# Compressed keys with the tokens held stationary, computed behind the first gates; their probabilities split in two ahead of the transposes

## The chip, the cores and the metric

The kernel runs on one core of one Trainium2 chip. The core has a tensor engine (PE in the profile, with its weight loads listed apart as PEld), VectorE (DVE), ScalarE (ACT), GpSimd (POOL), and SyncE (SP), whose queue issues all the DMAs of this kernel. Each engine works through its own queue in order and waits on semaphores of the others. The metric is the device time of one execution in microseconds (us).

## The reference

Two layers of a decoder trunk over 512 tokens of width 1024, in float32. In each layer one projection feeds four mixers; the outputs are gated, concatenated, projected and added to the residual. The change touches mixer B, which has three branches: attention over compressed blocks of keys, over selected blocks, and over a window. With 512 tokens, 16 selected blocks of 64 and a window of 512, the second and third branch see every earlier token. The compressed branch is this:

```python
cmp_idx = cmp_start[:, None] + jnp.arange(CMP_LEN)[None, :]      # 31 blocks of 32 tokens, 16 apart

def compress(tok, w):
    blocks = tok[:, cmp_idx] + pe_cmp
    return blocks.reshape(B, n_cmp, CMP_LEN * HEAD_DIM) @ w

k_cmp = rope(compress(kc_tok, w_cmp_k)[:, :, None], cmp_end, ROT_DIM)[:, :, 0]
v_cmp = compress(vc_tok, w_cmp_v)
...
s_c = jnp.einsum('bqhd,bnd->bhqn', qb, k_cmp) * scale
p_c = masked_softmax(s_c, valid_c)
o_c = jnp.einsum('bhqn,bnd->bqhd', p_c.astype(dtype), v_cmp)
...
return g[..., 0:1] * o_c + g[..., 1:2] * o_s + g[..., 2:3] * o_w
```

## The kernel before

Tokens are cut into four tiles of 128. Large products run in float32r; to keep float32 accuracy both operands are split into a high and a low part, and three of the four products are added (`lin_tok`, lines 137 to 139, with the tokens stationary; `lin_ch`, lines 147 to 149, with the weights stationary and all 512 tokens moving). Weights come in groups through four staging buffers `st`; ACT rounds them to the high part `wh` (line 122), POOL subtracts to get the low part `wl` (line 95).

A layer first runs the projections of queries, keys, values and of an indexer, as a software pipeline over tiles. Then come, in the order of the source: `compress`, the gates of mixer A (`gates("a", 0)`, `gates("a", 1)`), the gates of mixer B, attention of both mixers tile by tile with the top-k search `topk` (lines 341 and 342, long chains of MAX8 and MATCH_REPLACE8 on DVE) and the convolution and pooling mixers in between, and last the output projection.

The order within each engine's queue is not the order of the source. A list scheduler places the instructions by its own estimate of time, with the source's order as priority; so a change of one step can move rows far from it, and rows of later steps fill the gaps of earlier ones.

`compress` projects the tokens to compressed-branch keys and values (one `lin_ch`). It loads the position term `pe_cmp` by a DMA, transposes it on PE (line 443) and copies it to `pe` on DVE (line 445). ACT copies the projection into two buffers `u` (one for keys, one for values) in which each column holds a token and the token 16 further on; POOL adds `pe` to each (line 463). Then line 467 multiplies: for keys and for values 16 products each, with a 128x64 piece of the weight `st` stationary and 32 columns of `u` (every 16th) moving, into 64 rows of a bank `ms`. These are float32 products, and the profile lists each as two instructions. ACT copies the result to `kv`, PE transposes it back (line 473), and ACT and DVE make `zc` (keys, rotated in lines 262 to 265) and `vc` (values, high and low part, 32 rows). `zc` is transposed (line 480) into the first 32 columns of the window keys `kTB`.

In `att_b(i)` the 32 compressed probabilities of four heads end up in `e` (128 tokens x 4 x 32). Line 590 transposes each head's 32 columns; ACT rounds the 32x512 result to `ph` (line 593), DVE subtracts to get `pl`, and two products with 32 rows each (lines 595 and 596) add to the bank `pv` that already holds the other two branches. Scores of a head (lines 509 and 510) go into one of two banks `s`; DVE reads them (line 513), ACT takes the exponential (line 515). A gate's `lin_ch` goes into one of two banks `mm`, which DVE frees with line 493.

Of the kernel before, what the change touches and what calls it, by code (L numbers as in the profile page):

```python
# [28 lines left out]
BIG = 10  # places for tiles of [P, T]  # L29
WARM = 28  # products on nothing at the start  # L30
# [4 lines left out]
# first columns of the parts of w_in  # L35
A_Q, A_V, A_QI, A_KI, A_GATE, B_Q, B_KC, B_KS, B_GATE, C_B, C_GATE = 0, 320, 384, 640, 680, 936, 1192, 1320, 1588, 1844, 2612

# columns of the table of shape constants
# [27 lines left out]
def trunk(ctx: ExitStack, tc: tile.TileContext, x, norm_w, w_in, w_out, conv_w, pe_cmp, w_cmp_k, w_cmp_v,  # L66
# [26 lines left out]
    def lo(eng, dst, src, hi):  # L93
        """dst = src - hi, the part of src that its rounding to float32r left out."""
        eng.tensor_sub(dst, src, f(hi))  # L95

# [1 line left out]
    def load_w(src, segs, early=None, start=False):  # L98
        """segs: (first column, columns) runs of src that make up one group; by quarters of its rows.
        early: tag of a place that is still free for the loads; start: the first group of all"""  # L100
# [28 lines left out]
    def lin_tok(ps, act, i, w, c0, n, order=range(KC)):  # L129
        """ps[:, :n] = act (tokens of tile i) @ w[:, c0:c0+n]"""  # L130
# [10 lines left out]
    def lin_ch(act, w, c0):  # L141
        """(w[:, c0:c0+128])^T @ act^T : 128 channels by all tokens"""
# [31 lines left out]
    # the tensor engine's clock rises only after some microseconds of work: done on nothing while the loads run  # L174
# [13 lines left out]
    psh = const.tile([P, DEPTH, 2], F32, name="psh")  # L188
    x1d = dp.tile([T, DM], F32, name="x1d")

    def first_loads(h):
        """the other loads, between those of the first group of weights"""
# [25 lines left out]
    def mean_sq(xp, acc):  # L218
        """acc (EPS to begin with) and the part of the mean of squares that the columns xp make up"""
# [9 lines left out]
    def rms(xt, g, ms=None):  # L229
        """xt, g: by halves of the columns; ms: mean of xt's squares"""  # L230
# [21 lines left out]
    def rope(eng, z, n, half, tb, rows=P):  # L252
        """z: [rows, n, d], rotated in place; tb: [rows, 4*half] = cos, cos, -sin, sin"""
# [13 lines left out]
    def pipeline(tasks, depth=4):  # L267
        """Starts a task with each round, and takes each of those under way a step further."""
# [17 lines left out]
    def layer(l, hT, w_first, norm):  # L286
        """hT: the layer's normalized input, transposed, w_first: its first group of weights; norm, if any, writes
        the tiles of hT. Returns the like for the next layer."""
# [12 lines left out]
        def group_idx(i, w):  # L301
            """indexer queries of tile i, and the scores of its tokens against those before"""
# [8 lines left out]
            # rows of qiT[h % 4]: high, high, low part of the queries; of kiT: high, low, high part of the keys  # L311
# [37 lines left out]
        # keys of the selected and of the window branch; the compressed ones stand before the latter  # L349
# [4 lines left out]
        def stack_q(m, i, pq):  # L354
            """pq: two heads a transpose; even heads as (high, low), odd ones as (low, high) rows"""
# [61 lines left out]
        def group_bq(i, w):  # L417
            """queries of the second mixer, values of the first"""
# [16 lines left out]
        kcT = [kTB[s][:, 1, 0:32] for s in range(2)]  # L435
        vc = res.tile([32, P], F32R, name=nm("vc"), tag="vc")

        def compress(w):
# [6 lines left out]
            V.tensor_copy(pe, pt[:, 0:16])  # L445
            pc = bank("ms", 1)
            us = []
            wts = []
            for s, wsrc in enumerate((w_cmp_k, w_cmp_v)):
# [14 lines left out]
                us.append(u)  # L464
            for s in range(2):
                for t in range(16):
                    PE.matmul(pc[0:HD, s * 32 : (s + 1) * 32], wts[2 * s + t // 8][:, t % 8, :], us[s][:, t::16],  # L467
                              start=t == 0, stop=t == 15)
            kv = sm.tile([HD, 2, 32], F32, name=nm("kv"), tag="kv", bufs=1)
# [86 lines left out]
        def att_b(i):  # L556
# [32 lines left out]
            for h in range(NH):  # L589
                PE.transpose(pt[0:32, h * P : (h + 1) * P], e[:, h, :], ident)  # L590
# [200 lines left out]
```

## Time and profile before

| | |
|---|---|
| median of 3 runs | 576.3 us (573.21 to 577.37) |
| span of the profiled execution | 577.7 us; no time of it outside the span is listed |
| busy: PE, PEld, DVE, ACT, POOL | 542.4, 473.1, 448.9, 318.3, 296.0 us |
| DMA | 51.14 MB, mean 89 GB/s |
| HBM | 46.33 MB read, 4.19 MB written |

The profile is one execution; times in it are us from the start of the span unless marked ns. Busy time of PE is modelled and overlaps (matmuls are pipelined), so the distance between the starts of two matmuls is the better measure of what one costs. The chain of waits follows the work that ended last back from the end. A view of windows gives, for each stretch of time, how long each engine was busy and the clock that PE was granted, as a share of full speed.

### The profile page before, as it was taken

The page shows a single profiled execution, that of the slowest core. Times are in us where ns is not written, and L with a number is a line of the kernel's source. Part 1 is how long each engine was busy: PE and PEld are TensorE (multiplying, and loading weights), DVE is VectorE, ACT ScalarE, POOL GpSimd, SP SyncE. Part 2 cuts the span into 40 slices and gives each one's busy share as a digit, 9 for nine tenths or more (in the row PEclk, how much of TensorE's full clock was granted, in tenths as well). Part 3 has the DMA queues.
Part 4 walks back from the last instruction along what each step waited for, and adds up shares of the span by engine and source line. Part 5 has one row for each costly group of instructions (what it writes and reads, how often), then busy time and mean ns, then how long its engine had stood idle before and what let it go on. Part 6 is the DMA issues. An engine that isn't in the chain of part 4 may idle for free.

```text
span 577.7 us, 9703 instructions
## 1 busy us (share of the span) xinstructions
PE 542.4 (94%) x3088; PEld 473.1 (82%) x3088; DVE 448.9 (78%) x1154; ACT 318.3 (55%) x787; POOL 296.0 (51%) x394
## 2 busy tenths in 40 slices
PE   5989799798999999999999989989999999999995
PEld 4989697676878877699999978768788887869895
DVE  4867899799999977762275769987999997897523
ACT  3457855253547566663455595536454756565433
POOL 4755641364546194643675455326554639273342
PEclk9899999799999999999999999987999999999999
DMA  8632311283222020526531512116513212123303
GB/s 260 192 94 54 74 34 23 56 209 83 54 56 65 28 79 13 147 91 198 147 117 48 141 35 64 37 37 178 134 30 81 64 48 58 52 88 114 111 1 145
DMA packets 70370, 51.14 MB, mean 89 GB/s; under 512 B 19248, under 2 KB 64432, under 8 KB 70320
## 3 DMA queue, kind: packets, MB, share of 16 engines
q1 hardware_dynamic: 70320, 50.54, 31.8%
q8 instruction: 24, 0.39, 0.3%
q14 instruction: 26, 0.21, 0.1%
HBM read 46.33 MB, written 4.19 MB: 87 GB/s over the span
## 4 chain that ended last, share of the span: by engine, by line
PE 67%; DVE 22%; ACT 4%; POOL 2%; issue 2%; DMA 2%; SPq 1%; POOLq 0%; ACTq 0%; DVEq 0%
PE mm L139 9%; PE mm L137 9%; PE mm L138 8%; PE mm L147 7%; PE mm L148 7%; PE mm L149 7%; PE tr L529 4%; DVE acc L342 4%; DVE acc L331 4%; DVE m L341 3%; PE ms L467 2%; PE s L509 2%; PE s L510 2%; PE pv L535 2%; PE pv L534 2%
## 5 line engine op out<-in xcount | busy, mean ns | idle before, releaser
L95 POOL TENSOR_TENSOR wl<-st,wh 128x768 fp32r<-128x768 f32 (+4 forms) x94 | 159.2, 1713 | 63.2 <-ACT wh L122 51.2
L147 PE MATMUL mm<-hT,wh 128*128 128x512 f32 x272 | 110.1, 405 | 3.8 <-DVE sg L493 3.0
L149 PE MATMUL mm<-hT,wl 128*128 128x512 f32 x272 | 108.2, 399 | 0.0
L148 PE MATMUL mm<-hT,wh 128*128 128x512 f32 x272 | 108.1, 399 | 0.0
L522 POOL TENSOR_SCALAR pb<-pb,rs 128x512 f32<-128x512 f32 (+3 forms) x96 | 53.7, 577 | 98.8 <-DVE rs L519 39.0
L515 ACT ACTIVATE pb<-pb,mn 128x512 f32<-128x512 f32 (+3 forms) x96 | 53.7, 559 | 72.1 <-DVE mn L513 71.6
L122 ACT ACTIVATE wh<-st 128x768 fp32r<-128x768 f32 (+4 forms) x92 | 70.7, 775 | 25.4 <-DMA st<-in_w_in_dram 9.2
L137 PE MATMUL mm<-wh,hT 128*128 128x360 f32 (+3 forms) x240 | 74.8, 313 | 8.1 <-ACT hT L248 4.3
L139 PE MATMUL mm<-wh,hT 128*128 128x360 f32 (+3 forms) x240 | 74.7, 312 | 0.9 <-DVE hT L95 0.9
L138 PE MATMUL mm<-wl,hT 128*128 128x360 f32 (+3 forms) x240 | 74.1, 310 | 0.0
L147 PEld LDWEIGHTS mm<-hT,wh 128*128 128x128 f32 x272 | 51.8, 191 | 14.2 <-DVE sg L493 3.5
L137 PE MATMUL mm<-wh,mT 128*128 128x384 f32 (+1 forms) x192 | 61.7, 323 | 0.3 <-ACT mT L604 0.3
L139 PE MATMUL mm<-wh,mT 128*128 128x384 f32 (+1 forms) x192 | 61.1, 320 | 0.6 <-DVE mT L95 0.6
L138 PE MATMUL mm<-wl,mT 128*128 128x384 f32 (+1 forms) x192 | 61.4, 320 | 0.0
L148 PEld LDWEIGHTS mm<-hT,wh 128*128 128x128 f32 x272 | 51.9, 191 | 9.7 <-issue 0.4
L149 PEld LDWEIGHTS mm<-hT,wl 128*128 128x128 f32 x272 | 51.4, 189 | 10.1 <-issue 0.5
L95 DVE TENSOR_TENSOR pl<-tr,ph 128x512 fp32r<-128x512 f32 (+1 forms) x68 | 45.9, 681 | 15.3 <-ACT ph L532 14.0
L137 PEld LDWEIGHTS mm<-wh,hT 128*128 128x128 f32 x240 | 46.1, 193 | 9.7 <-ACT hT L248 4.8
L341 DVE MAX8 m<-acc 128x8 f32<-128x384 f32 (+2 forms) x96 | 52.1, 552 | 0.4
L342 DVE MATCH_REPLACE8 acc<-m,acc 128x384 f32<-128x384 f32 (+2 forms) x96 | 52.0, 543 | 0.1
L139 PEld LDWEIGHTS mm<-wh,hT 128*128 128x128 f32 x240 | 46.1, 192 | 1.7 <-DVE hT L95 1.7
L138 PEld LDWEIGHTS mm<-wl,hT 128*128 128x128 f32 x240 | 46.2, 193 | 0.2
(194 smaller groups left out, 1171.5 us busy)
## 6 DMA issues: line engine op xcount, KB each, us to landing
st<-in_w_in_dram SPq DMA_DIRECT2D x104, 128.0 KB, 2.8
st<-in_w_in_dram SPq DMA_DIRECT2D x28, 256.0 KB, 3.0
st<-in_w_out_dram SPq DMA_DIRECT2D x16, 384.0 KB, 3.3
x<-in_x_dram SPq DMA_DIRECT2D x16, 256.0 KB, 4.1
st<-in_w_in_dram SPq DMA_DIRECT2D x8, 320.0 KB, 4.8
st<-in_w_out_dram SPq DMA_DIRECT2D x8, 256.0 KB, 3.0
x1d<-x SPq DMA_DIRECT2D x8, 256.0 KB, 2.4
x<-x1d SPq DMA_DIRECT2D x8, 256.0 KB, 3.3
```

Source lines behind the costliest of these rows:

```text
L95: eng.tensor_sub(dst, src, f(hi))
L122: S.activation(wh[:, :, :n], st[:, :, :n], AF.Copy)
L137: PE.matmul(ps[:, :n], act[0][:, k, ts], rh, start=st, stop=False)
L138: PE.matmul(ps[:, :n], act[0][:, k, ts], rl, start=False, stop=False)
L139: PE.matmul(ps[:, :n], act[1][:, k, ts], rh, start=False, stop=sp)
L147: PE.matmul(ps, lh, act[0][:, k, :], start=k == 0, stop=False)
L148: PE.matmul(ps, lh, act[1][:, k, :], start=False, stop=False)
L149: PE.matmul(ps, ll, act[0][:, k, :], start=False, stop=k == KC - 1)
L341: V.max(m8, a)
L342: V.match_replace(a, m8, a, MARK)
L515: S.activation(p, p, AF.Exp, scale=-1.0, bias=mn[:, h : h + 1], accum_out=rs[:, h : h + 1])
L522: G.tensor_scalar(p, p, rs[:, h : h + 1], 0.0, op0=OP.mult, op1=OP.add)
```

## The change

- In `compress`, `pe` is copied by ACT (line 451 now) and no longer by DVE. The function ends after the additions to `u` and returns the buffers.
- A new function `compressed` holds the products and what follows. It is called behind `gates("a", 0)` and `gates("a", 1)`.
- The products change sides: 32 columns of `u` are stationary, and the 64 columns of the weight move. The result has the 32 compressed tokens in its rows, 64 columns for keys and 64 for values, so `kv` and the two transposes back are gone, and `zc` and `vc` are read from the bank directly.
- `vc` grows from 32 to 96 rows: the values (high and low part), the same again, and 32 rows of zeros.
- In `att_b`, ACT rounds `e` into the first 32 columns of `es`, and DVE puts the rest into the next 32; a third 32 columns stay zero. Four transposes of 96 columns give the high part, the low part and zeros in 96 rows; one ACT copy makes `ph` of them, and one product with 96 rows stands for the two with 32.
- Two buffers `es` are set to zero at the start, in POOL's queue between the two steps that make `ident`; comments and docstrings are gone, so line numbers grow by 4 to 7.

```diff
+    e_split = [const.tile([P, NH, 96], F32, name=f"es{s}") for s in range(2)]
+    for t_ in e_split:
+        G.memset(t_[:, :, HD:96], 0.0)
...
-        vc = res.tile([32, P], F32R, name=nm("vc"), tag="vc")
+        vc = res.tile([96, P], F32R, name=nm("vc"), tag="vc")
+        G.memset(f(vc[HD:96]), 0.0)
...
-            V.tensor_copy(pe, pt[:, 0:16])
-            pc = bank("ms", 1)
+            S.activation(pe, pt[:, 0:16], AF.Copy)
...
+            return wts, us
+
+        def compressed(wts, us):
+            pc = bank("ms", 1)
             for s in range(2):
                 for t in range(16):
-                    PE.matmul(pc[0:HD, s * 32 : (s + 1) * 32], wts[2 * s + t // 8][:, t % 8, :], us[s][:, t::16],
+                    PE.matmul(pc[0:32, s * HD : (s + 1) * HD], us[s][:, t::16], wts[2 * s + t // 8][:, t % 8, :],
                               start=t == 0, stop=t == 15)
-            kv = sm.tile([HD, 2, 32], F32, name=nm("kv"), tag="kv", bufs=1)
-            S.activation(kv, pc[0:HD, 0:HD].rearrange("p (s n) -> p s n", s=2), AF.Copy)
-            pz = bank("tr", 2)
-            for s in range(2):
-                PE.transpose(pz[0:32, s * HD : (s + 1) * HD], kv[:, s, :], ident[0:HD, 0:HD])
             z = sm.tile([32, 2, HD], F32, name=nm("zc"), tag="zc", bufs=1)
-            S.activation(z, pz[0:32, None, 0:HD].to_broadcast([32, 2, HD]), AF.Copy)
-            S.activation(vc[:, 0:HD], pz[0:32, HD:P], AF.Copy)
-            lo(V, vc[:, HD:P], pz[0:32, HD:P], vc[:, 0:HD])
+            S.activation(z, pc[0:32, None, 0:HD].to_broadcast([32, 2, HD]), AF.Copy)
+            S.activation(vc[0:32, 0:HD], pc[0:32, HD:P], AF.Copy)
+            lo(V, vc[0:32, HD:P], pc[0:32, HD:P], vc[0:32, 0:HD])
+            S.activation(vc[32:HD], f(vc[0:32]), AF.Copy)
             rope(V, z, 2, 8, tab[0:32, TBC : TBC + 32], rows=32)
...
+            S.activation(es[:, :, 0:32].bitcast(F32R), e, AF.Copy)
+            V.tensor_sub(es[:, :, 32:HD], e, es[:, :, 0:32])
             pt = bank("tr", 2)
             for h in range(NH):
-                PE.transpose(pt[0:32, h * P : (h + 1) * P], e[:, h, :], ident)
+                PE.transpose(pt[0:96, h * P : (h + 1) * P], es[:, h, :], ident)
             ph = wk.tile([P, T], F32R, name=nm("ph"), tag="ph", bufs=3)
-            pl = wk.tile([P, T], F32R, name=nm("pl"), tag="pl", bufs=2)
-            S.activation(ph[0:32], pt[0:32], AF.Copy)
-            lo(V, pl[0:32], pt[0:32], ph[0:32])
-            PE.matmul(po, vc, ph[0:32], start=False, stop=False)
-            PE.matmul(po, vc, pl[0:32], start=False, stop=True)
+            S.activation(ph[0:96], pt[0:96], AF.Copy)
+            PE.matmul(po, vc, ph[0:96], start=False, stop=True)
...
-        compress(w)
+        cmp_in = compress(w)
         gates("a", 0, w, P)
         gates("a", 1, w, 2 * P)
+        compressed(*cmp_in)
```

The scheduler places rows anew, so the order in the queues says more than the source. First PE in layer 0, at the products of the compressed keys and values (`ms`); `s` are scores of mixer B's last tile, the `mm` rows belong to the gates of mixer B, `kv` is the result that before was transposed back. Before:

```order
L509 MATMUL s_1528<-kTB_180,qb_1235 128x512
L510 MATMUL s_1528<-kTB_181,qb_1235 128x512
L467 MATMUL ms_1301<-u_1308,st_1302 64x32 x8
L467 MATMUL ms_1301<-u_1308,st_1305 64x32 x8
L509 MATMUL s_1533<-kTB_180,qb_1235 128x512
L510 MATMUL s_1533<-kTB_181,qb_1235 128x512
L467 MATMUL ms_1301<-u_1319,st_1313 64x32 x8
L467 MATMUL ms_1301<-u_1319,st_1316 64x32 x8
L509 MATMUL s_1538<-kTB_180,qb_1235 128x512
L510 MATMUL s_1538<-kTB_181,qb_1235 128x512
L147 MATMUL mm_1454<-hT_135,wh_1432 128x512
```

And now:

```order
L515 MATMUL s_1529<-kTB_184,qb_1240 128x512
L516 MATMUL s_1529<-kTB_185,qb_1240 128x512
L477 MATMUL ms_1383<-st_1306,u_1312 32x64 x8
L477 MATMUL ms_1383<-st_1309,u_1312 32x64 x8
L477 MATMUL ms_1383<-st_1317,u_1323 32x64 x8
L477 MATMUL ms_1383<-st_1320,u_1323 32x64 x8
L515 MATMUL s_1534<-kTB_184,qb_1240 128x512
L516 MATMUL s_1534<-kTB_185,qb_1240 128x512
L515 MATMUL s_1539<-kTB_184,qb_1240 128x512
L516 MATMUL s_1539<-kTB_185,qb_1240 128x512
L147 MATMUL mm_1455<-hT_139,wh_1433 128x512
```

The products stand at the same place of PE's queue in both: behind the gates of mixer A and the first head's scores. The scheduler had put them there before, too. What differs is that the values' products now follow the keys' at once, and the second head's scores come after both. The fourth head's scores (`s_1544`) now stand 16 rows after the last row shown.

Next ACT at the same place; `pe` is the position term, `sg` the gates of mixer A, `rl` and the `acc` behind it belong to the indexer. Before:

```order
L492 ACTIVATE sg_1400<-mm_1375 128x512
L330 ACTIVATE rl_900<-s_898 128x512
L330 ACTIVATE rl_905<-s_903 128x512
L492 ACTIVATE sg_1400<-mm_1403 128x512
L330 ACTIVATE rl_910<-s_908 128x512
L515 ACTIVATE pb_1522,rs_1527<-pb_1522,mn_1526 128x512
```

And now:

```order
L498 ACTIVATE sg_1353<-mm_1328 128x512
L334 ACTIVATE rl_905<-s_903 128x512
L334 ACTIVATE rl_910<-s_908 128x512
L451 ACTIVATE pe_1304<-tr_1302 128x16
L498 ACTIVATE sg_1353<-mm_1356 128x512
L334 ACTIVATE rl_915<-s_913 128x512
L521 ACTIVATE pb_1523,rs_1528<-pb_1523,mn_1527 128x512
```

The copy of `pe` is new in ACT's queue, between the third `rl` and the second gate.

Last DVE behind the second gate of mixer A: ISA rows with `s` read a head's scores (line 513 before, 519 now), `r` and `zc` are the rotation of the compressed keys. Before, from the third head's scores on (the second head's row stands five rows ahead of the first shown):

```order
L513 ISA pb_1524,mn_1526<-s_1538,mask 128x512
L513 ISA mn_1526 128x1
L341 MAX m_475_2157<-acc_771 128x8
L343 TENSOR_SCALAR acc_680<-acc_680 128x256
L341 MAX m_476_2191<-acc_842 128x8
L513 ISA pb_1525,mn_1526<-s_1543,mask 128x512
L513 ISA mn_1526 128x1
L342 MATCH_REPLACE acc_771<-m_475_2157,acc_771 128x384
L262 TENSOR_TENSOR r_287_1365<-zc_1361,tab 32x32
L263 TENSOR_TENSOR r_288_1366<-zc_1361,tab 32x2x8
L95 TENSOR_TENSOR vc_183<-tr_1358,vc_183 32x64
L264 TENSOR_TENSOR r_288_1366<-zc_1361,tab 32x2x8
```

And now:

```order
L499 SCALAR_TENSOR_TENSOR sg_1353<-sg_1353,mm_1356 128x512
L346 MATCH_REPLACE acc_685<-m_372_1754,acc_685 128x256
L335 SCALAR_TENSOR_TENSOR acc_847<-rl_915,wi_551,acc_847 128x512
L345 MAX m_470_2155<-acc_776 128x8
L345 MAX m_372_1754<-acc_685 128x8
L346 MATCH_REPLACE acc_776<-m_470_2155,acc_776 128x384
L346 MATCH_REPLACE acc_685<-m_372_1754,acc_685 128x256
L266 TENSOR_TENSOR r_288_1421<-zc_1416,tab 32x32
L267 TENSOR_TENSOR r_289_1422<-zc_1416,tab 32x2x8
L95 TENSOR_TENSOR vc_187<-ms_1383,vc_187 32x64
L268 TENSOR_TENSOR r_289_1422<-zc_1416,tab 32x2x8
L519 ISA pb_1524,mn_1527<-s_1534,mask 128x512
```

The rotation has moved from behind the fourth head to ahead of the second, and the copy of `pe` has left DVE's queue. From the attention on the rows of all engines are placed anew.

More of the change, by code (lines that the diff above doesn't have):

```diff
@@ L558, in att_b @@
             e = sm.tile([P, NH, 32], F32, name=nm("e"), tag="e", bufs=2)
+            es = e_split[i % 2]
             mx = sm.tile([P, NH], F32, name=nm("mx"), tag="mx", bufs=2)
```

## The prediction

> **What bounds the kernel now.** I read the page first (busy shares, the granted clock, the chain of waits), then who waits for whom on PE, then windows of the two stretches where the change sits, and last the queues of single engines there. The page:
>
> ```profile
> span 577.7 us, 9703 instructions
> PE 542.4 (94%) x3088; PEld 473.1 (82%) x3088; DVE 448.9 (78%) x1154; ACT 318.3 (55%) x787; POOL 296.0 (51%) x394
> PEclk9899999799999999999999999987999999999999
> PE 67%; DVE 22%; ACT 4%; POOL 2%; issue 2%; DMA 2%; SPq 1%; POOLq 0%; ACTq 0%; DVEq 0%
> ```
>
> PE bounds the span, DVE is second. The clock of PE is full except at two places behind the start, the eighth slice and the 27th and 28th. PE's own waits name what lies there:
>
> ```profile
> PE ms L467 <- POOL u L463: 5.2, 2, 3.0
> PE mm L147 <- DVE sg L493: 3.0, 2, 2.9
> ```
>
> The products of the compressed keys wait for POOL once in each layer (3.0 us, and so 2.2 us in the other). The second row is a wait on the gates of mixer B that DVE has to finish. Windows (length, then busy us of PE, PEld, DVE, ACT and POOL with counts, then the granted clock, the DMA share and GB/s), layer 0 first:
>
> ```profile
> 104.00:107.00 3.00, 0.03 (x1) 0.03 (x1) 3.00 (x12) 0.60 (x1) 1.69 (x2) 1.00 0.00 0
> 107.00:107.80 0.80, 0.80 (x14) 0.80 (x15) 0.80 (x2) 0.00 (x0) 0.80 (x1) 1.00 0.00 0
> 108.00:118.00 10.00, 10.00 (x60) 8.26 (x59) 6.37 (x19) 4.44 (x10) 3.94 (x4) 0.50 0.51 127
> 118.00:133.00 15.00, 12.51 (x55) 9.66 (x54) 15.00 (x31) 8.10 (x16) 10.98 (x9) 1.00 0.77 191
> 133.00:197.00 64.00, 63.59 (x326) 52.63 (x327) 63.39 (x177) 32.75 (x79) 28.58 (x31) 1.00 0.24 60
> 197.00:240.00 43.00, 42.50 (x215) 33.86 (x214) 32.08 (x100) 29.14 (x71) 27.68 (x37) 1.00 0.19 50
> 385.00:397.50 12.50, 12.50 (x71) 10.64 (x71) 7.45 (x23) 5.62 (x13) 4.86 (x5) 0.50 0.49 124
> 398.00:410.00 12.00, 11.82 (x53) 9.00 (x52) 12.00 (x29) 7.20 (x13) 10.14 (x10) 1.00 0.71 178
> 410.00:477.00 67.00, 67.00 (x344) 55.78 (x343) 65.76 (x194) 37.59 (x89) 31.75 (x35) 1.00 0.27 66
> 477.00:520.00 43.00, 42.46 (x211) 32.96 (x210) 36.49 (x88) 27.44 (x65) 28.60 (x34) 1.00 0.23 68
> ```
>
> Two things count here. Behind each wait PE runs at half clock, for 10 us in layer 0 and 12.5 us in layer 1. And DVE, full before and after, has its only long idle there: 10.00 - 6.37 = 3.63 us and 12.50 - 7.45 = 5.05 us. From 118 to 197 and from 398 to 477 DVE has next to nothing free. So what PE gains in the two stretches is worth only what DVE can follow; later, from 197 and 477 on, DVE has 11 and 6.5 us free and PE bounds alone. The Trainium skill ("TensorE: Matmul & The Clock Gate", Part 1) has the clock fall to half after an idle window of about 3.4 us and return after a busy one; the trace agrees as far as it goes, with 3.0 us of wait ahead of a fall to 0.50.
>
> **The wait and the half clock.** Why POOL is late, in layer 0, from the queues of PE, ACT, DVE and POOL:
>
> ```profile
> 100.78 0.23 PE L443 MATMUL tr<-ident,pet 16*128 16x16 f32 x1
> 100.60 0.60 ACT L330 ACTIVATE rl<-s 128x512 f32<-128x512 f32 x1 [0.73 <-DVE acc L331]
> 104.96 0.17 DVE L445 COPY pe<-tr 128x16 f32<-128x16 f32 x1
> 105.31 2.84 POOL L463 TENSOR_TENSOR u<-u,pe 128x512 f32<-128x512 f32 x2 [14.10 <-DVE pe L445]
> 103.59 0.39 PE L510 MATMUL s<-kTB,qb 128*128 128x512 f32 x1
> 106.97 2.95 PE L467 MATMUL ms<-u,st 128*64 128x32 f32 x32 [3.00 <-POOL u L463]
> 111.00 3.62 PE L467 MATMUL ms<-u,st 128*64 128x32 f32 x32
> ```
>
> The transpose of `pet` is done at 101.0, but its copy is queued on DVE behind top-k steps until 104.96; POOL has waited 14.1 us for it. Now the copy is third behind the gate on ACT, right behind the `rl` that ends at 101.2. POOL's two additions (2.84 us together) then end near 102.9 and 104.3, and PE, at its place at 104.0, finds the first `u` ready; the second is needed only half way. The wait goes in both layers, and with it what lets the clock fall. That the source puts the products behind the gates moves nothing on PE (same place in both queues); ACT's copy is what does it.
>
> The products themselves: at full clock 14 in 0.80 us, 0.057 us each; at half clock 3.62 / 32 = 0.113. The new ones load 32 columns and move 64, the old ones loaded 64 and moved 32. No row shows that shape. Nearest below: nothing saved or lost, 0.057. Nearest above: the four transposes with a 32-column load, (167.47 - 167.12) / 4 = 0.09 us each, with 128 columns moving.
>
> ```profile
> 167.12 0.60 PE L590 MATMUL tr<-ident,e 128*32 128x128 f32 x4
> 167.47 0.38 PE L509 MATMUL s<-kTB,qb 128*128 128x288 f32 x1
> ```
>
> I take 0.06: 64 instructions in 3.8 us, done by 107.8 in layer 0 against 114.6. At 0.09 they take 5.8 us, which the slack below still covers.
>
> PE's side of the gain: the wait, and half of the time at half clock: 3.0 + 5.0 = 8.0 us and 2.2 + 6.25 = 8.5 us, 16.5 in all. That is the upper bound. DVE's side is its idle: 3.63 + 5.05 = 8.7 us. What is late next is DVE: the rotation of the compressed keys now stands ahead of its reading of the second head. In layer 0 it takes
>
> ```profile
> 119.54 1.29 DVE L262 TENSOR_TENSOR r<-zc,tab 32x32 f32<-32x32 f32 x1
> 124.36 0.07 DVE L342 MATCH_VALUE_LOAD acc<-m,acc 128x8 f32 x1
> 132.64 0.67 DVE L493 SCALAR_TENSOR_TENSOR sg<-sg,mm 128x512 f32<-128x512 f32 x1
> 408.85 0.66 DVE L493 SCALAR_TENSOR_TENSOR sg<-sg,mm 128x512 f32<-128x512 f32 x1
> ```
>
> 4.8 us, the first two rows apart. So the second head's bank `s` is freed only near 116.5 (about 111 for the rows ahead, plus 4.8, plus 0.6), PE stands there at the fourth head's scores for some 3 us after the 16 gate rows between, and behind it PE has 35 rows to go, 35 x 0.23 = 8.1 us, to 124.6. DVE, never idle, reaches the first gate of mixer B at 132.64 - 3.63 = 129.0 (layer 1: 408.85 - 5.05 = 403.8). PE is ready some 4 us before. By the clock gate's rule in the Trainium skill this new wait could halve the clock for one more window, 1.7 us of work lost; those 4 us would hold that, so the sum does not change. I therefore take DVE's side, **8.7 us**, with 16.5 as the far end; the near end is 0, if DVE's idle only moves to the wait for `zc`.
>
> The lost transposes of `kv` and its copy lie in the same stretch and are worth nothing beyond this. So is the copy of `vc` on ACT (44% busy there).
>
> **The 96-row product.** Before and beside:
>
> ```profile
> 172.30 0.39 PE L149 MATMUL mm<-hT,wl 128*128 128x512 f32 x1
> 172.62 0.50 PE L595 MATMUL pv<-ph,vc 32*128 32x512 f32 x1
> 173.05 0.40 PE L509 MATMUL s<-kTB,qb 128*128 128x288 f32 x1
> 87.34 0.39 PE L148 MATMUL mm<-hT,wh 128*128 128x512 f32 x1
> 87.57 0.40 PE L328 MATMUL s<-kiT,qiT 96*128 96x512 f32 x1
> 87.80 0.40 PE L149 MATMUL mm<-hT,wl 128*128 128x512 f32 x1
> ```
>
> Usual starts are 0.23 us apart. The 32-row product starts 0.32 behind its neighbour and the next 0.43 behind it: 0.32 + 0.43 - 0.23 = 0.52 us for one. A product with 96 rows (the indexer's) fits into the usual 0.23. Two at 0.52 become one at 0.23: 0.81 us for each of 4 tiles in 2 layers, **6.5 us**, where PE is full. The four transposes load 96 columns for 32; the rows of line 529 with 128 columns are no slower, so nothing. If the 96 rows paid the 32-row price it would be 0.52 x 8 = 4.2. The Trainium skill ("TensorE: Matmul & The Clock Gate", "Why this matters for your kernels") says that one product with K = 32 takes the time of one with K = 128; the trace disagrees (0.50 against 0.39 us, and the starts). By that rule one product of 0.23 would go per tile, 1.8 us.
>
> **The split ahead of the transposes.** DVE subtracts 128x128 where it subtracted 32x512, ACT gets one copy more:
>
> ```profile
> L578 DVE TENSOR_TENSOR e<-e,mx x8: 268/292/294, 144.3 to 494.2; 128x128 f32<-128x128 f32 x8
> L579 ACT ACTIVATE e<-e x8: 294/302/312, 144.6 to 494.8; 128x128 f32<-128x128 f32 x8
> L95 DVE TENSOR_TENSOR pl<-tr,ph 32x512 fp32r<-32x512 f32 x8 | 5.4, 671 | 0.0
> ```
>
> DVE saves (0.67 - 0.29) x 8 = 3.0 us, ACT pays 8 x 0.30 = 2.4 at half load. `e` was finished some 12 us ahead of its transposes (153.8 to 167.1 in the first tile), which hides the two steps; without that cover each tile would pay 0.6. The DVE saving makes room for PE's in the stretches where both are full, and I count it only as that.
>
> **The sum.** 8.7 + 6.5 = 15.2. From the span: 577.7 - 15.2 = 562.5. The median of the runs is 1.4 below the span, so I predict 561.
>
> **The rivals.**
> - *A. The 96 rows cost what 32 did, or the 32-row price is another's.* 8.7 + 1.8 to 4.2: 567 to 564 in span, 565 as a time with the median's offset. Against it stands line 328. 0.10.
> - *B. The stall only moves.* DVE stops at the rotation because `zc` is late, PE at the fourth head, the clock falls again, and of the 8.7 nothing is left: 577.7 - 6.5 - 1.4, 570. For it: DVE's queue is in order, and the rotation is now early. Against it: `zc` is ready near 109 (products to 107.8, then a copy), DVE comes to it near 111. 0.13.
> - *C. DVE is no bound.* What PE needs of DVE is not the whole queue, since top-k steps can be placed later; all of 16.5 comes: 577.7 - 23 - 1.4, 553. Against it: DVE's queue is full and the rows that PE waits for stand in it at nearly the same place. 0.10.
> - *D. The narrow or strided stationary operand is dear, and the kernel slower.* The weight load now takes 32 columns, every 16th of `u`; so far only moving operands were read with that step. If a product with a quarter of the array pays what the 32-row one did, 0.43 instead of 0.06, that is 64 x 0.37 = 24 us a layer. About 4 us go into PE's slack, 20 are late at the gates of mixer B, 40 in both layers, less 15.2: 600. It turns the balance from (4 + 7.6) / 64 = 0.18 more, that is 0.24 us per instruction. Against it: the transposes with a 32-column load at 0.09. 0.05.
> - *E. The new order of the attention costs.* All rows behind the gates are placed anew; a few waits like the 2.9 us on `sg` would take 8 or more of the gain: 570 to 578. No row speaks for one more than another. 0.10.
>
> **How the numbers follow.** The forecast has 0.52, its own range 557 to 566. The range from 553 (C) to 572 (B and half of E) leaves out D, half of E and what is under C, under 0.2. One per cent, about what can be told from no change, is 570.5 and 582 here. Faster by over 1%: the forecast, A, C and 0.10 of B: 0.82, less 0.02 for what none of these names: 0.80. Within 1%: the rest of B and most of E, 0.13. Slower: D, and a little of E, 0.07.
>
> **What would show it.** Right: no wait of the `ms` products on POOL; POOL's additions near 101.4; no DVE idle of over a microsecond between 102 and 129; the start of the first convolution matmul near 129 against 133.37; the 96-row product at 0.39 us with the next start 0.23 behind. A wait at the fourth head's scores may show and costs nothing. Wrong: DVE idle ahead of `zc` (B), `ms` starts over 0.2 us apart (D), 0.43 behind the 96-row product (A), PE idle in 133 to 240 (E).

## The result, and the profile after

The changed kernel takes 570.9 us (median of 10 runs, 568.3 to 573.8) against 576.2 us before (10 runs, 572.5 to 579.0): a ratio of 0.9906 with a 95% interval of 0.9881 to 0.9931, so 5.4 us. The forecast was 561, within 553 to 572. The time lies near the upper edge of that range; of the 15.2 us a third came. Two executions at a granted clock of 0.56 and 0.85 (862.9 and 598.0 us) are left out of the ratios below.

The page of the profile after, the lines that answer to those of before:

```profile
span 569.5 us, 9672 instructions
PE 533.6 (94%) x3076; PEld 469.3 (82%) x3076; DVE 449.4 (79%) x1152; ACT 319.8 (56%) x797; POOL 298.9 (52%) x398
PEclk8899989998999999999999989999999999999999
PE 60%; DVE 26%; ACT 5%; DMA 3%; issue 2%; POOL 1%; SPq 1%; POOLq 0%; ACTq 0%; DVEq 0%
```

The long half clock of layer 1 (slices 27 and 28 before) is gone, and that of layer 0 shows in the tenth slice; the other dents lie in the projections, which the change does not touch. The execution of this profile took 571.2 us, 1.7 over its span. The same offset puts the profile of before (span 577.7) at about 579.4, 3 us above its median. The forecast had put the median 1.4 us below the span and sized its terms on an execution that was slower than most; so both kernels were profiled once more (below).

The view of PE's waits, after. No product of the compressed keys waits for POOL any more; these stand in its place:

```profile
PE ms L578 <- DVE kTB L95: 1.7, 1, 1.7
...
PE ms L667 <- DVE rs L523: 1.5, 1, 1.5
...
PE ms L667 <- DVE cd L661: 1.1, 1, 1.1
```

The first is at the gates of mixer B: the compressed scores of the last tile wait for the compressed keys. The other two are among the last rows of a layer, where PE had no wait of that length before. The timelines of ACT, POOL, PE and DVE in layer 0 (start, length, instruction):

```profile
102.58 0.18 ACT L451 ACTIVATE pe<-tr 128x16 f32<-128x16 f32 x1 [0.72 <-PE tr L449]
102.91 2.98 POOL L468 TENSOR_TENSOR u<-u,pe 128x512 f32<-128x512 f32 x2 [11.34 <-ACT pe L451]
105.44 3.89 PE L477 MATMUL ms<-st,u 128*32 128x64 f32 x64
109.26 0.50 PE L515 MATMUL s<-kTB,qb 128*128 128x512 f32 x1
...
124.67 0.18 PE L577 MATMUL ms<-kTB,qb 128*128 128x32 f32 x1
126.28 0.17 DVE L95 TENSOR_TENSOR kTB<-tr,kTB 128x32 fp32r<-128x32 f32 x1
126.51 0.28 PE L578 MATMUL ms<-kTB,qb 128*128 128x32 f32 x1 [1.66 <-DVE kTB L95]
127.44 0.66 DVE L499 SCALAR_TENSOR_TENSOR sg<-sg,mm 128x512 f32<-128x512 f32 x1
...
171.37 0.39 PE L147 MATMUL mm<-hT,wh 128*128 128x512 f32 x1
171.60 0.40 PE L602 MATMUL pv<-ph,vc 96*128 96x512 f32 x1
171.83 0.60 PE L535 MATMUL tr<-ident,pb 128*128 128x128 f32 x4
```

POOL starts right behind ACT's copy, and the 64 products run without a wait, (109.26 - 105.44) / 64 = 0.060 us each. The 96-row product starts 0.23 behind its neighbour, and the next row 0.23 behind it. DVE reaches the first gate of mixer B at 127.4. Counted from the first product of the gates, which comes 1.6 us later than before (86.40 against 84.80), each of these is as forecast or earlier. What is not: PE stands 1.66 us at the compressed scores, and a stretch of half clock follows, with PE busy nearly all the time (length, busy us of PE, PEld, DVE, ACT, POOL with counts, clock, DMA share, GB/s):

```profile
127.20:130.61 3.41, 3.05 (x9) 2.46 (x10) 3.41 (x10) 0.22 (x1) 3.41 (x4) 0.50 0.45 111
```

### The profile page after: what moved, and what is told of

It is laid out like the page before. It is cut to its first block, busy times and chain, and to the rows that moved or that the text cites. A ratio compares the mean times of both kernels' runs of the same rounds, so it can differ in the third digit from the quotient of the medians.

```text
span 569.5 us, 9672 instructions
## 1 busy us (share of the span) xinstructions
PE 533.6 (94%) x3076; PEld 469.3 (82%) x3076; DVE 449.4 (79%) x1152; ACT 319.8 (56%) x797; POOL 298.9 (52%) x398
## 4 chain that ended last, share of the span: by engine, by line
PE 60%; DVE 26%; ACT 5%; DMA 3%; issue 2%; POOL 1%; SPq 1%; POOLq 0%; ACTq 0%; DVEq 0%
PE mm L137 9%; PE mm L139 9%; PE mm L138 8%; PE mm L147 7%; PE mm L149 7%; PE mm L148 7%; DVE acc L346 4%; DVE m L345 4%; DVE acc L335 4%; PE tr L535 3%; PE pv L541 2%; PE pv L540 2%; PE s L516 2%; PE s L515 2%; ACT wh L122 2%
## 5 line engine op out<-in xcount | busy, mean ns | idle before, releaser
L95 POOL TENSOR_TENSOR wl<-st,wh 128x768 fp32r<-128x768 f32 (+4 forms) x94 | 161.1, 1734 | 73.6 <-ACT wh L122 63.8
L149 PE MATMUL mm<-hT,wl 128*128 128x512 f32 x272 | 108.3, 400 | 0.8 <-POOL wl L95 0.8
L137 PE MATMUL mm<-wh,hT 128*128 128x360 f32 (+3 forms) x240 | 76.0, 319 | 7.8 <-ACT hT L252 4.2
L139 PE MATMUL mm<-wh,hT 128*128 128x360 f32 (+3 forms) x240 | 75.9, 316 | 1.2 <-DVE hT L95 1.2
L149 PEld LDWEIGHTS mm<-hT,wl 128*128 128x128 f32 x272 | 51.7, 190 | 11.7 <-POOL wl L95 1.7
L137 PEld LDWEIGHTS mm<-wh,hT 128*128 128x128 f32 x240 | 47.3, 198 | 9.4 <-ACT hT L252 4.7
L139 PEld LDWEIGHTS mm<-wh,hT 128*128 128x128 f32 x240 | 47.2, 197 | 2.0 <-DVE hT L95 2.0
L95 DVE TENSOR_TENSOR pl<-tr,ph 128x512 fp32r<-128x512 f32 x60 | 40.6, 683 | 10.2 <-ACT ph L538 10.1
```

What stands on the lines that cost most here:

```text
L137: PE.matmul(ps[:, :n], act[0][:, k, ts], rh, start=st, stop=False)
L139: PE.matmul(ps[:, :n], act[1][:, k, ts], rh, start=False, stop=sp)
L149: PE.matmul(ps, ll, act[0][:, k, :], start=False, stop=k == KC - 1)
```

## How the loss is measured

Each layer is cut into three windows: 50 us from the first product of the gates (`L149`), then up to the last product of gates and convolution, then up to the middle of the output projection. In each, idle is the length less PE's busy time, the loss by half clock is the length times one less the granted clock (rounded to 0.01, so within 0.25 us for 50), and the rest is PE at work at full clock. The rest leans on the modelled busy time and also moves with the spacing of the rows: it differs by 1.3 us between the two executions of before, and by up to 3.5 us between kernels with the same products. The first and third window of each layer, before (length, then busy us of PE, PEld, DVE, ACT, POOL with counts, clock, DMA share, GB/s):

```profile
84.80:134.80 50.00, 44.15 (x219) 35.25 (x219) 45.99 (x113) 22.19 (x46) 22.95 (x22) 0.90 0.39 95
...
237.20:270.00 32.80, 32.51 (x210) 29.04 (x210) 20.88 (x48) 18.71 (x44) 16.84 (x19) 1.00 0.47 152
362.80:412.80 50.00, 47.57 (x228) 38.21 (x227) 44.54 (x123) 24.16 (x50) 23.34 (x26) 0.86 0.37 92
...
512.30:551.80 39.50, 38.36 (x210) 34.08 (x209) 25.44 (x58) 20.24 (x47) 16.86 (x20) 1.00 0.32 104
```

And after:

```profile
86.40:136.40 50.00, 47.21 (x245) 37.36 (x244) 49.47 (x131) 23.55 (x50) 25.60 (x23) 0.93 0.46 111
...
228.00:268.40 40.40, 37.47 (x237) 32.84 (x236) 26.66 (x65) 22.48 (x54) 15.47 (x21) 1.00 0.41 128
361.40:411.40 50.00, 47.77 (x262) 38.21 (x261) 49.58 (x140) 26.79 (x59) 25.09 (x26) 1.00 0.45 110
...
497.80:543.70 45.90, 42.41 (x235) 37.53 (x234) 31.44 (x70) 23.04 (x53) 17.52 (x23) 1.00 0.32 98
```

At the gates the loss falls: idle from 5.85 + 2.43 = 8.3 us to 2.79 + 2.23 = 5.0, half clock from 0.10 x 50 + 0.14 x 50 = 12.0 to 0.07 x 50 = 3.5, and DVE is busy 49.5 of the 50 us. At the ends of the layers idle rises from 0.29 + 1.14 = 1.4 us to 2.93 + 3.49 = 6.4.

All profiles cut in this way, both layers together, us. Ratios are to the kernel before in the same comparison, with their 95% intervals; the profile of a kernel is one of its runs, whose time stands beside it.

| kernel | ratio | time of the profiled run | gates: idle, half clock | later: idle in the middle, at the ends, half clock | rest |
|---|---|---|---|---|---|
| before | 1 | 579.4 (estimate) | 8.3, 12.0 | 0.5, 1.4, 0 | 351.9 |
| before, again | 0.9997 [0.9972, 1.0022] | 572.8 | 6.6, 5.0 | 0.5, 1.1, 0 | 353.2 |
| after | 0.9906 [0.9881, 0.9931] | 571.2 | 5.0, 3.5 | 0.9, 6.4, 0 | 348.4 |
| after, again | 0.9899 [0.9862, 0.9936] | 571.2 | 5.2, 3.5 | 1.0, 6.5, 0 | 348.5 |
| copy on ACT | 0.9819 [0.9789, 0.9849] | 563.5 | 3.7, 0 | 0.6, 1.0, 0 | 353.2 |
| sides | 0.9912 [0.9885, 0.994] | 568.3 | 4.9, 1.5 | 0.7, 3.3, 0 | 353.2 |
| copy and sides | 1.0047 [1.002, 1.0073] | 577.7 | 6.7, 1.5 | 1.2, 6.9, 1.8 | 354.8 |
| 96 rows | 1.0063 [1.0029, 1.0097] | 584.2 | 4.4, 14.0 | 1.6, 7.9, 1.8 | 346.5 |
| copy and 96 rows | 0.9835 [0.9778, 0.9892] | 569.0 | 4.1, 3.0 | 5.0, 0.3, 1.9 | 347.2 |
| sides and 96 rows | 0.9845 [0.9801, 0.9889] | 566.7 | 5.1, 1.5 | 3.2, 3.8, 0 | 346.6 |
| after, keys on DVE | 0.9833 [0.9792, 0.9873] | 569.7 | 5.0, 3.5 | 2.7, 1.2, 3.9 | 346.8 |
| copy on ACT, keys on DVE | 0.9945 [0.9913, 0.9977] | 576.5 | 4.6, 5.0 | 0.4, 5.6, 0 | 354.0 |
| after, rotation on POOL | 0.9762 [0.9729, 0.9796] | 563.9 | 5.4, 5.0 | 1.0, 1.4, 0 | 345.0 |

The rows from the copy on ACT to sides and 96 rows are parts of the change; the last three are small edits that move the order.

## The experiments

**The kernel before once more.** No edit.

> The kernel before once more, for a second profile and for the clock of each of its runs. Theory S (the first profile of before was a slow execution): times run about 1.7 us above their spans, so the span of 577.7 belongs to a time of about 579.4, 3 us above the median. Then the clock of the runs varies by more than 0.005, the time falls as the clock rises, and a run near the median shows one half-clock stretch fewer or a shorter one (about 3 us less lost than the 5.1 + 6.8 us of the first profile). Rival R (the first profile is typical): both half-clock stretches of 10 us and more stand in the new profile too, and the clock is the same in all runs.

Measured: 576.2, the same; its twelve runs have clocks of 0.968 to 0.981, with 579.3 us at 0.972 and 572.8 at 0.981. The profile is of the fastest run. Its two windows at the gates:

```profile
85.30:135.30 50.00, 47.17 (x260) 37.84 (x259) 49.33 (x132) 24.80 (x52) 25.56 (x23) 1.00 0.45 111
...
356.60:406.60 50.00, 46.18 (x229) 36.98 (x228) 45.16 (x123) 24.07 (x51) 23.49 (x26) 0.90 0.37 92
```

In layer 0 the clock did not fall at all, with 2.8 us of idle. The wait itself is there in both layers, 4.1 us against 5.2 in the first profile:

```profile
PE ms L467 <- POOL u L463: 4.1, 2, 2.2
```

Theory S holds as far as two profiles go: the wait is in both, the half clock behind it in layer 0 is in the first alone. This one is of a fast run, where the theory asked for one near the median. The loss at the gates was 20.3 us in the first profile and 11.6 here.

**After once more.** No edit.

> After once more, for a second profile. Theory T (the loss at the end of each layer belongs to the order and comes in every execution, while the half clock comes and goes): idle of PE behind the last product of the convolution again 2.9 and 3.5 us, within 0.5, and a pause before the compressed scores again, while the loss by half clock at the gates differs from 3.2 and 0 us. Rival (the end of the layers varies from run to run like the clock): 1.5 us or less of idle in one of the two layers.

Measured: 571.1. The ends of the layers lose 3.0 and 3.4 us (2.9 and 3.5 in the first profile). So that loss belongs to the order of the rows and comes each time. The pause before the compressed scores is 1.7 us again. The clock fell at the same place too, with the same 3.5 us of loss, so the last part of theory T missed: this pair does not show that the clock varies.

**The copy on ACT alone.**

```diff
-            V.tensor_copy(pe, pt[:, 0:16])
+            S.activation(pe, pt[:, 0:16], AF.Copy)
```

> Before, with the copy of the position term on ACT and nothing else. Theory S (most of what the whole change gives is this copy): the waits of 3.0 and 2.2 us on POOL are gone, and the time is 3 to 6 us under before, 570 to 573. Rival P (the step of the prediction): DVE's idle of 3.6 and 5.1 us is taken up whole, 8.7 us, 567.5. Rival M (the pause only moves to the compressed scores of the last tile, which wait for the keys): less than 2 us, 574 to 576.

Measured: 565.8, 10 us under before, twice what the whole change gives. The rows of its four windows:

```profile
84.50:134.50 50.00, 48.08 (x263) 38.11 (x261) 49.62 (x135) 25.99 (x55) 25.82 (x23) 1.00 0.44 111
...
229.80:261.30 31.50, 31.40 (x205) 28.44 (x204) 17.54 (x43) 17.44 (x40) 16.79 (x20) 1.00 0.54 164
354.30:404.30 50.00, 48.24 (x263) 38.23 (x262) 49.62 (x138) 26.48 (x57) 24.79 (x26) 1.00 0.44 109
...
497.90:535.90 38.00, 37.11 (x206) 33.69 (x205) 22.92 (x51) 18.69 (x44) 16.14 (x20) 1.00 0.35 109
```

The step of the forecast is right: wait and half clock go, DVE's idle is used (49.6 of 50 us busy in both layers), 8.7 us were forecast. The theory that the copy gives 3 to 6 us was too low; rival P, the step of the forecast, gave 567.5. The profile is of the fastest of the six runs (563.5 us), so the 3.7 us of loss in the table may be below what is usual. And the ends of the layers lose no more than before (1.0 us).

**The sides alone.** Columns of `u` stationary, the rest of the change left out (copy on DVE, two products with 32 rows). The call stands behind the gates, as in after.

```diff
-                    PE.matmul(pc[0:HD, s * 32 : (s + 1) * 32], wts[2 * s + t // 8][:, t % 8, :], us[s][:, t::16],
+                    PE.matmul(pc[0:32, s * HD : (s + 1) * HD], us[s][:, t::16], wts[2 * s + t // 8][:, t % 8, :],
...
-            kv = sm.tile([HD, 2, 32], F32, name=nm("kv"), tag="kv", bufs=1)
...
```

> Before, with the sides of the compressed products changed and nothing else (copy of the position term on DVE, two products with 32 rows). Theory W (the half clock lasted 10 to 14 us because the products moved only 32 columns; with 64 columns it comes back after one window): the waits of some 2 us on POOL stay, the half clock costs 1.7 us or nothing in a layer where it cost 5 to 7, and the time is 567 to 571. Rival (the step of the prediction: the copy on ACT is what gives the gain): 575 to 577, as before.

Measured: 571.6 (0.9912), 0.6 us over the range of theory W. The wait is still there, in the view of PE's waits of this kernel:

```profile
PE ms L473 <- POOL u L464: 4.3, 2, 2.4
```

That is 4.3 us in two waits, against 5.2 before, but at the gates the half clock costs 1.5 us instead of 5.0 to 12.0. The profile is of the fastest of eleven runs, but the others bear it out: their granted clock over the whole span is 0.979 to 0.989, that of the sixteen runs of before beside them 0.967 to 0.976. The reason is in the time after the wait. In these traces a stretch of half clock lasts 3.41 us or two, three or four times that, so the windows here are 3.41 us long. Before, in layer 1, with the products of the compressed keys alone (length, busy us of PE and PEld with counts, clock):

```profile
380.89:384.30 3.41, 0.17 (x3) 0.18 (x4) 1.00 0.00 0
384.30:387.72 3.42, 3.34 (x32) 3.20 (x31) 0.50 0.20 33
387.72:391.13 3.41, 1.56 (x15) 1.56 (x16) 0.50 0.46 125
391.13:394.54 3.41, 2.07 (x20) 1.93 (x19) 0.50 0.38 86
394.54:397.95 3.41, 0.00 (x0) 0.00 (x0) 0.50 0.91 247
```

And the same wait with the new sides (the kernel with sides and 96 rows, below):

```profile
374.90:378.31 3.41, 0.32 (x5) 0.32 (x6) 1.00 0.00 0
378.31:381.72 3.41, 3.10 (x31) 2.86 (x28) 0.50 0.25 59
381.72:385.13 3.41, 2.05 (x32) 1.92 (x32) 1.00 0.43 110
```

With 32 moving columns PE is issuing all the time and still stays at half clock through three such windows; the clock comes back only behind a window with none of them. With 64 columns it comes back after one window that is nearly full of them. The other profiles fit: behind this wait the half clock lasts 10 to 14 us in all five stretches with 32 columns (two before, one in its repeat, two with the 96 rows alone) and 3.4 us in both with 64 columns. The Trainium skill ("TensorE: Matmul & The Clock Gate", Part 1) has the clock return after one busy window of about 3.4 us; the trace agrees for 64 columns; with 32 columns the windows above, in which PE is busy throughout, do not bring it back.

**Copy and sides, without the 96 rows.** After, with two products of 32 rows as before.

```diff
-            S.activation(ph[0:96], pt[0:96], AF.Copy)
-            PE.matmul(po, vc, ph[0:96], start=False, stop=True)
+            S.activation(ph[0:32], pt[0:32], AF.Copy)
+            lo(V, pl[0:32], pt[0:32], ph[0:32])
+            PE.matmul(po, vc, ph[0:32], start=False, stop=False)
+            PE.matmul(po, vc, pl[0:32], start=False, stop=True)
...
```

> After, without the split probabilities and the 96-row product (two products with 32 rows each as before, values in 32 rows). Prediction: the 96 rows are worth 6.5 us, so this kernel takes 577. Theory S (PE saves 0.81 us a tile there, but the last tiles of a layer wait for the chain of transposes, copies and products, which the saving does not shorten): 571 to 573, at most 2 us over after.

Measured: 577.8, slower than before by 0.5%. The number of the prediction came out, theory S fell: from here to after, the 96 rows bring 6.4 us of PE's rest (354.8 to 348.4) and all of it reaches the end. But two parts that give 10 and 5 us alone give a loss together. The gates lose no more than with the sides alone by half clock (1.5 us), 1.8 us more by idle; the ends of the layers lose 6.9 us and 1.8 by half clock.

**The 96 rows alone.** Before, with the split and the 96-row product; the values are written into 96 rows.

```diff
...
-            PE.matmul(po, vc, ph[0:32], start=False, stop=False)
-            PE.matmul(po, vc, pl[0:32], start=False, stop=True)
+            PE.matmul(po, vc, ph[0:96], start=False, stop=True)
```

> Before, with the split probabilities and the 96-row product alone (the compressed keys and values computed as before, the values written three times into 96 rows). Prediction: 6.5 us under before, 569.7. Theory S: 0 to 3 us under before, 573 to 576, with the product itself at 0.23 us between starts and new idle of PE near the end of each layer.

Measured: 578.7 (1.0063): both expectations missed. PE's rest is 346.5 us, 6 us under that of before, but the ends lose 7.9 us and both half-clock stretches are there. The profile is of one of the slowest of the twelve runs (584.2 us), so its 14.0 us of half clock are more than usual.

**Sides and 96 rows.** After, with the copy back on DVE.

```diff
-            S.activation(pe, pt[:, 0:16], AF.Copy)
+            V.tensor_copy(pe, pt[:, 0:16])
```

> After, with the copy of the position term back on DVE. In PE's queue 19 and 22 pv products stand behind the last product of the convolution. Theory T: the waits on POOL and the half clock behind them are back, 8 to 10 us, and the end of the layers is 2 to 3 us better: 576 to 579. Rival C (the copy is worth 10 us only in the old order, and after has already another wait in its place): 570 to 572.

Measured: 568.4 (0.9845 [0.9801, 0.9889]), no slower than after and perhaps faster: the intervals just touch. Theory T missed: the waits on POOL are back (4.1 us in two), but as with the sides alone the half clock costs only 1.5 us, and the pause at the compressed scores is gone. Rival C was nearer, and still 2 us too high. So the copy on ACT, the better of the two parts alone, is worth nothing once the sides are changed.

**Copy and 96 rows.** The copy on ACT on top of the 96 rows, in two runs; the profile is of the second.

> Before, with the copy of the position term on ACT and the 96-row product, the compressed products as they were. The copy alone gave 565.8. In PE's queue 17 and 19 products of the attention (pv) stand behind the last product of the gates and the convolution in the two layers, where after has 24 and 24 and the copy alone 18 and 20. Theory T (what after loses stands at the end of each layer, where the attention is left alone): this kernel keeps a short end and saves the 5.5 to 6 us of PE work of the 96 rows, 560. Rival N (the 96 rows bring nothing when they are put on a kernel that is not the tuned one, as in the run of them alone): 565 to 568.

> The copy on ACT and the 96-row product once more, since the profile of its first run came from a disturbed execution (clock 0.56). Time 565 to 568 again. Theory N2 (the 96 rows save 5.5 to 6 us of PE work here too, and idle of PE and half clock take it back): work of PE in the mixers 5 us under that of the copy alone, idle and loss of clock 5 us over it. Rival (the work is not saved in this order): work within 2 us of the copy alone.

Measured: 0.9816 [0.9771, 0.9861] and 0.9835, no better than the copy alone (0.9819). Theory T missed, N2 holds: the rest is 6.0 us lower (353.2 to 347.2), but idle and half clock are 9 us higher, 4.4 us of it idle in the middle of the layers.

**One copy of 32 columns, on after and on the copy alone.** The high part of the compressed keys, 128x32, is copied by DVE and no longer by ACT. PE's work stays the same.

```diff
-            S.activation(kcT[0], pk[:, 0:32], AF.Copy)
+            V.tensor_copy(kcT[0], pk[:, 0:32])
```

> After, with one copy of 32 columns (the high part of the compressed keys) on DVE and no longer on ACT. The scheduler answers with 15 and 19 pv products behind the last convolution product, where after has 24 and 24. Theory T: idle of PE behind that product falls from 2.9 + 3.5 us to 1.5 or less in sum, and the time to 562 to 566. Rival G (after loses at the gates alone, by the pause of 1.7 us at the compressed scores and the half clock behind it): the end of the layers stays as it is, and the time is 567 to 569 if the pause goes, 571 if it doesn't.

> Before with the copy of the position term on ACT (565.8), and the same copy of 32 columns on DVE as in the run of after. Here the scheduler answers with 26 and 30 pv products behind the last convolution product, where the copy of the position term alone has 18 and 20. The work of PE is the same, and the keys are ready earlier. Theory T: the end of the layers loses 4 us or more to idle, and the time is 570 to 574. Rival G: 564 to 566, no slower than without it.

Measured: 0.9833 against 0.9906 of after, 0.7% faster; and 0.9945 against 0.9819 of the copy alone, 1.3% slower. The same edit, one way and the other. The intervals of the second pair are apart; those of the first are apart against the ten runs of after and touch that of its repeat (0.9862 to 0.9936). The two windows at the ends of the layers, first after with the keys on DVE:

```profile
235.60:267.00 31.40, 30.61 (x200) 27.71 (x199) 18.40 (x42) 15.84 (x35) 13.00 (x14) 1.00 0.54 171
...
504.70:542.10 37.40, 36.96 (x209) 34.09 (x208) 23.74 (x50) 18.71 (x43) 16.60 (x20) 1.00 0.35 110
```

and the copy on ACT with the keys on DVE, with its windows at the gates:

```profile
86.90:136.90 50.00, 47.64 (x247) 37.59 (x246) 48.57 (x132) 24.10 (x51) 25.65 (x23) 0.93 0.45 111
...
228.80:269.90 41.10, 38.42 (x238) 32.57 (x237) 27.59 (x66) 22.00 (x52) 15.66 (x20) 1.00 0.40 125
362.20:412.20 50.00, 47.71 (x255) 37.70 (x254) 49.59 (x139) 26.00 (x55) 25.06 (x26) 0.97 0.44 110
...
500.20:548.90 48.70, 45.74 (x254) 39.79 (x254) 32.83 (x89) 24.42 (x57) 16.77 (x25) 1.00 0.27 91
```

In the first the ends lose 1.2 us instead of 6.4, in the second 5.6 instead of 1.0. For the second kernel theory T holds, by the ends and by the time (573.5 us), and rival G falls; the half clock at the gates adds 5.0 us in the profiled run. For the first, T holds for the ends but not for the time: 568.1 us is over its 562 to 566 and within G's 567 to 569. G's condition is not met, though: the pause at the compressed scores is shorter (1.1 us) but not gone, and the loss at the gates is the same 8.5 us. What the ends gave (5.2 us) the middle of the layers took back in the profiled run, 1.8 us more of idle and 3.9 of half clock.

**The rotation on POOL.** After, with the rotation of the compressed keys on the other engine.

```diff
-            rope(V, z, 2, 8, tab[0:32, TBC : TBC + 32], rows=32)
+            rope(G, z, 2, 8, tab[0:32, TBC : TBC + 32], rows=32)
```

> After, with the rotation of the compressed keys on POOL and no longer on DVE (some 4.8 us of DVE's queue at the gates in each layer). Behind the last product of the convolution stand 16 and 21 pv products, after has 24 and 24. Theory T (end of the layers) with DVE as the bound at the gates: 4 to 6 us at the gates and 3 us at the ends of the layers, 562 to 565. Rival (POOL, which rounds the weights there, becomes the next wait): 567 or more, with PE waiting for wl.

Measured: 562.1 (0.9762), the fastest of all and faster than both kernels. The time is what theory T gave, the place only half: the ends lose 1.4 us instead of 6.4 and the rest is 3 us lower, but at the gates 10.4 us are lost, no less than in after. Why the rest is lower with the same products stays open. The rival missed.

## Why the prediction was wrong

**By terms.** The means of the two profiles on either side, with the rest read as above: the mixers of both layers took 370.4 us before and 364.5 after, 5.9 less, close to the 5.4 of the medians.

| | forecast | measured |
|---|---|---|
| gates: wait and half clock | -8.7 | 16.0 to 8.6: -7.4 |
| 96 rows, as PE's rest | -6.5 | 352.6 to 348.5: -4.1 |
| middle and ends of the layers | 0 | 1.8 to 7.4: +5.6 |

The forecast was sized on the first profile of before. Against that one the gates gave about 12 us, against the second about 3; so that the mean comes near 8.7 is in part luck.

**The step that failed** is in "The sum": "8.7 + 6.5 = 15.2", which takes every us that PE saves to be saved at the end, on the ground that "later, from 197 and 477 on, DVE has 11 and 6.5 us free and PE bounds alone". In this order PE does not bound alone there. It finishes gates and convolution, the work that can fill a gap, 10.8 us sooner behind the first product of the gates in layer 0 (228.0 - 86.4 against 237.2 - 84.8; 3.5 us sooner than in the second profile of before) and 13 us in layer 1 (against either profile). Some 25 products more are left behind that point (237 and 235 in the third windows against 210 and 210), rows of attention and pooling, and they wait for DVE, 5 us of idle more. PE's waits in the two third windows of after:

```profile
PE ms L667 <- DVE cd L661: 1.1, 1, 1.1
PE pv L541 <- DVE pl L95: 1.0, 2, 0.8
PE pv L540 <- DVE om L549: 0.5, 1, 0.5
...
PE ms L667 <- DVE rs L523: 1.5, 1, 1.5
PE mm L139 <- DVE mT L95: 0.9, 1, 0.9
```

That is rival E, "The new order of the attention costs", to which the forecast gave 0.10, with "No row speaks for one more than another". Rows were there to be read: behind the last of these products PE's queue has 24 and 24 products `pv` after, and 20 and 20 before. That count is no law: with copy and sides alone 16 in layer 1 go with 4.3 us of idle, with the 96 rows alone 17 with 6.6. What the runs show is that the loss is of the order (the same in two executions, made and removed by one small copy); which rule of the scheduler makes it stays open.

**Gates.** The size is near in the mean and the reason half right. The copy on ACT does what the forecast says and gives more than forecast when it is alone: 16.0 us of loss (mean of the two profiles of before) come down to 3.7 in its fastest run. But the sides, which the forecast priced at nothing, take most of the same loss by another way, the shorter half clock; the two do not add. And "what is late next" was not the fourth head's scores: it was the compressed scores, 1.66 us, because the low part of the keys stands behind top-k steps in DVE's queue. The forecast let PE's 4 us of slack cover the half clock behind such a pause ("those 4 us would hold that"). In the trace the slack is not there: PE waits only 0.36 us at the gate of mixer B and then works through the half clock, which costs 3.5 us. This is rival B in small: after loses 8.6 us at the gates where the copy alone loses 3.7.

**The 96 rows.** Right: 0.23 us between starts, and in three pairs of kernels with the same other parts the rest falls by 6.0 (on the copy), 6.6 (on the sides) and 6.4 us (on both), 6.5 forecast. From before to after only 4.1 of it shows, since the rest is 354.8 with copy and sides, 2 us above before; the `pv` products and scores stand in wider spacings there (the scores 0.190 us apart in the mean against 0.178, idle left out), and no run told why. How much of the 6 reaches the end depends on what else is in the kernel: all of it on copy and sides, some 4 us on the sides (0.9912 to 0.9845), nothing on the copy or on before.

**The other rivals.** A is out by the spacing, D by the 0.060 us of the products. C is not out: the copy alone gave 10.4 us (8.7 to 12.2 by its interval), as much as DVE's idle of 8.7 or more.

**The place.** That the call stands behind the first gates does nothing: with the call left at its old place the rows of all five queues come in the same order as in after, so this was not run. The place of this call does not reach the queues; a changed operand or engine does.

## What to carry to other kernels

When a scheduler places the rows anew, a local gain of some us is worth what the new order leaves of it: here two edits worth 10 and 5 us alone cost 3 us together, and one copy of 32 columns took 0.7% off one kernel and put 1.3% on another. So price an edit by stages, and look at the end of each stage for what fills PE there: work without dependencies that is used up early can be missed later, as here. And before a term is sized, take a second profile: the loss by half clock at the gates differed by 7 us between two executions of the kernel before.

## What was not expected of the hardware

A short instruction on DVE can last as long as what POOL is doing. In after, layer 0, the rotation on DVE and a step on four columns, with POOL at the same time (timelines):

```profile
110.96 3.79 POOL L95 TENSOR_TENSOR wl<-st,wh 128x512 fp32r<-128x512 f32 x3 [5.07 <-DMA st<-in_w_in_dram]
112.23 1.30 DVE L267 TENSOR_TENSOR r<-zc,tab 32x16 f32<-32x16 f32 x1
122.10 3.66 POOL L95 TENSOR_TENSOR wl<-st,wh 128x768 fp32r<-128x768 f32 x2 [0.34 <-ACT wh L122]
122.15 1.84 DVE L522 TENSOR_SCALAR rs<-rs 128x4 f32<-128x4 f32 x1
```

That step over the whole kernel, in the view of its tile (min, median and max in ns):

```profile
L522 DVE TENSOR_SCALAR rs<-rs x24: 146/164/1843, 122.1 to 519.4; 128x4 f32<-128x4 f32 x24
```

It takes 0.16 us as a rule, and 1.84 where it starts at 122.15 beside the first of POOL's two instructions (3.66 / 2 = 1.83 us each). With the copy alone, where POOL was between two instructions, the rotation's first three steps took 0.15 to 0.17 us, and the fourth, beside POOL again, 1.36. So the forecast's 4.8 us for the rotation held such waits: before, its first three steps took 1.29 to 1.87 us while POOL worked. The Trainium skill ("SBUF — State Buffer", "Who interferes with whom") says that the two engines share a pair of ports which one of them holds for a whole instruction, and that an operation of DVE with two inputs there, or in a two-port mode, has to wait; the trace agrees for the rotation, whose steps have two inputs there. Whether the step on four columns, which has one, ran in such a mode no row shows.
